# The last eight merge gates in pairs, each pair by seven block products with mixed inputs and summed weights

## The chip, the cores and the metric

The kernel runs on one core of a Trainium2 chip. The metric is the time of one execution on the device in microseconds (us). The core has one matmul engine (PE, with its weight loads shown apart as PEld), a vector engine (DVE), an activation engine (ACT), a general engine (POOL) and a queue engine (SP), on which this kernel starts nearly all of its transfers. Each engine works through its own list of instructions in order and waits for the others by semaphores.

## The reference

One layer of a hybrid decoder on 576 tokens (512 of a prompt, 64 of eight sampled sequences), all in 32-bit floats, D = 1024. What matters here:

```python
z = rmsnorm(x, norm1_g) @ w_in            # (576, 1024) @ (1024, N_IN)
# z holds the inputs of both branches and, at its end, 2 x 1024 columns of gates
y_a = mlstm_branch(z) @ w_branch_m        # (576, 512) @ (512, 1024)
y_b = rwkv_branch(z) @ w_branch_r         # (576, 512) @ (512, 1024)
gates = sigmoid(z[..., G_START:])
merged = gates[..., :D] * y_a + gates[..., D:] * y_b
x = x + merged @ w_out
u = rmsnorm(x, norm2_g) @ f_up            # then a convolution, gelu, f_down, ...
```

The gates are sixteen tiles of 128 columns: eight for y_a and eight for y_b. The sigmoid is made from tanh(z/2): the kernel stores tanh(z/2) and later takes (tanh + 1) * y, with a factor of one half.

## The kernel before, in words

**Layout and products.** Activations lie transposed: 128 channels on the partitions, the 576 tokens along the free axis, in two halves of 288 columns (HF). A matrix of 1024 input channels is eight blocks of 128. PE multiplies in a shortened 32-bit type (fp32r), so each operand is split into a high part and a remainder: the high part `wh` of a weight tile by a cast on ACT (L169), the remainder `wl` by a subtraction on DVE (L170), and the same for activations (names ending in h and l). Each product is three matmuls, wh by xh, wh by xl and wl by xh (half_k, L190 to L193). `dense` (L174) makes one output tile of 128 columns: it loads the weights as two tiles of 128x512 (L168), splits them, and issues for each of the two halves 8 blocks x 3 = 24 matmuls into a PSUM bank `pd`.

**Seven products for eight.** In the later stage f_up (`up`, L1316 and on) two output tiles are made together by `seven` (L287). Two tiles, with their inputs taken in upper and lower four blocks and the two column halves, are a product of 2x2 blocks by 2x2 blocks, eight block products in the plain way. `seven` makes seven, with weights that are sums of weight tiles (`plus`, L298) and activations that are mixed from the four quarter blocks (`mixed`, L274), and additions on the results. Each block product is 4 blocks x 3 = 12 matmuls (L306), so a pair takes 84 matmuls instead of 96. `seven` leaves the last product to its caller as `last`, so that a caller can read a bank before it.

**The gates.** `gate(i)` (L1205) makes gate i with `dense` from the normalised input `xs1` (tiles xa0h, xa0l to xa7h, xa7l), takes tanh of half of it on ACT into a tile `gst`, and stores that to DRAM as d_th[i] (L1210). An even i is a gate of y_a, an odd one a gate of y_b.

**What sets the order.** PLAN (L31) is a string of steps, and the body is issued in its order: x, a, d, b, s, c are steps of the RWKV branch (the last is c3, whose last results are stored to d_y[4] to d_y[7] at L941), m0 to m3 the four mLSTM heads, g0 to g15 the gates, which give PE dense work between the steps of the branches. A scheduler then reorders the instructions by its own estimate of when operands are ready, and fixes a list for each engine. The tail of PLAN is "... g7 m3 g8 g9 ... g15": the eight last gates stand behind the last head m3, whose products and vector work run among them. In a head, products of weights and values (L1136) are copied to `hn` (L1137), normalised in a chain of small DVE operations (L1154 and around) and ACT operations (L1156), transposed back on PE (L1159), multiplied into `og` and stored to d_y[h]. Then come the matrices of the sampled sequences (tiles C0 and VS, L1183 to L1203).

**Behind the gates.** `load_split` (L1230) reads d_y[4] to d_y[7] back as `yin` (L1232) and splits each (ACT L198, DVE L199) into y0h, y0l to y3h, y3l. `gated` (L1235) makes the branch's product with `dense` (four blocks, 24 matmuls), reads d_th as `th` (L1238) and multiplies. First come the eight tiles of y_b from d_y[4] to d_y[7], then the eight of y_a from d_y[0] to d_y[3], each added to its partner: that is the merge.

**Memory.** `rp` is the RWKV part's pool, `mp` the mLSTM part's, `wp` that of the weights (six raw tiles `wr`, four of wh and of wl). A tag names a place, and a new tile in a tag waits until the former one's readers are done.

Of the kernel before, what the change touches and what calls it, by code (L numbers as in the profile page):

```python
# [15 lines left out]
P = 128  # L16
# [11 lines left out]
KSC = 128.0 ** -0.5  # L28
DEC = math.exp(-0.5)

PLAN = "x0 a0 d0 x1 b0 a1 d1 s0 c0 g0 m0 b1 g1 x2 a2 d2 s1 c1 m1 g2 b2 x3 a3 d3 g3 s2 c2 b3 g4 g5 s3 m2 g6 c3 g7 m3 g8 g9 g10 g11 g12 g13 g14 g15".split()  # L31


VEC = {}
# [61 lines left out]
def build(tc, nc, I, O):  # L96
    from contextlib import ExitStack

    V, S, G, TE, SY = nc.vector, nc.scalar, nc.gpsimd, nc.tensor, nc.sync
# [9 lines left out]
    with st0:  # L109
# [32 lines left out]
        def half(hf):  # L142
            return slice(hf * HF, (hf + 1) * HF)
# [127 lines left out]
            return xn  # L271


        def mixed(tiles, pl, b11, b12, b21, b22, k, T4):  # L274

            n1, n2, t3, n4 = (pl.tile([P, HF], F32, tag=t, name="tt", bufs=2) for t in ("u2", "u2", "u3", "u3"))
            V.tensor_tensor(n1, b11, b12, ALU.subtract)
            G.tensor_tensor(t3, b22, b12, ALU.subtract)
            V.scalar_tensor_tensor(n2, n1, -1.0, b22, ALU.mult, ALU.subtract)
            V.tensor_tensor(n4, n2, b21, ALU.add)  # L280
            for name, t, e in (("n2", n2, V), ("n1", n1, G), ("t3", t3, V), ("n4", n4, V)):
                h, l = (tiles[name + a][:, k, :] for a in "hl")
                S.copy(h, t)
                e.tensor_tensor(l, t, h, ALU.subtract)
                T4[name].append((h, l))

        def seven(srca, srcb, x4, sp):  # L287

            def parts(w):
                wh, wl = [wp.tile([P, 4, P], F32R, tag=t, name=t, bufs=WB) for t in ("wh", "wl")]
                S.copy(wh, w)  # L294
                V.tensor_tensor(wl, w, wh, ALU.subtract)  # L295
                return wh, wl

            def plus(a, b, e):  # L298
                t = sp.tile([P, 4, P], F32, tag="ws", name="ws", bufs=3)
                e.tensor_tensor(t, a, b, ALU.add)  # L300
                return t

            def prod(pm, w, xs, more=False):
                for k in range(4):
                    for i, (a, b) in enumerate(((0, 0), (0, 1), (1, 0))):
                        TE.matmul(pm[:, 0:HF], w[a][:, k, :], xs[k][b], start=not more and k == 0 and i == 0,  # L306
                                  stop=k == 3 and i == 2, skip_group_check=more)

            def tile(tag):
                return sp.tile([P, HF], F32, tag=tag, name=tag, bufs=2)  # L310

            a11, a21, a22, a12 = wdma8(srca, 0), wdma8(srcb, 0), wdma8(srcb, 4), wdma8(srca, 4)
            A, F, E, Dm = (bank("d", "pd") for _ in range(4))
            w11 = parts(a11)
            prod(A, w11, x4["b11"])
            u3 = tile("u3")
            S.copy(u3, A[:, 0:HF])
            s1 = plus(a21, a22, V)
            s2 = plus(s1, a11, V)
            prod(F, parts(s2), x4["n2"])  # L320
            u2 = tile("u2")
            V.tensor_tensor(u2, F[:, 0:HF], u3, ALU.add)
# [12 lines left out]
            return A, u2, E, Dm, u3, last  # L335
# [40 lines left out]
        with ExitStack() as stn:  # L376
# [44 lines left out]
            xr = []  # L421
# [44 lines left out]
        rp = pool(stR, "rwkv")  # L466
# [11 lines left out]
        m0 = mp.tile([4, NB], F32, name="m0")  # L478
# [43 lines left out]

        xwa = r_tile(12, "t1")
        S.activation(xwa[0:64, :], xwa[0:64, :], AF.Tanh)
        xw = rp.tile([P, T], F32R, name="xw")
        xa = rp.tile([P, T], F32R, name="xa")
# [678 lines left out]
        def gate(i):  # L1205
# [3 lines left out]
                S.activation(th[:, hf * HF:(hf + 1) * HF], pss[hf][:, 0:HF], AF.Tanh, scale=0.5)  # L1209
            SY.dma_start(d_th[i], th)  # L1210

        mlstm_rows()
        for step in PLAN:
            (rwkv_in, rwkv_prep, rwkv_diag, rwkv_mid, rwkv_smp, rwkv_out, mlstm_head, gate)["xadbscmg".index(step[0])](int(step[1:]))
        SY.dma_start(O["o_shift"], o_shift)
        SY.dma_start(O["o_mconv"], o_mconv)

# [5 lines left out]
        x1 = [rpool.tile([P, T], F32, name=f"res{m}") for m in range(8)]  # L1223
# [43 lines left out]
        xn0 = [kp.tile([P, HF], F32, name=f"xn0{k}") for k in range(KD)]  # L1267
# [25 lines left out]
        fp = pool(stf_, "ffn")  # L1293
# [22 lines left out]
        def up(j):  # L1316
# [68 lines left out]
        for m in range(2):  # L1385
            hl = [fp.tile([P, 8, P], F32R, tag="x4", name="wg", bufs=8) for _ in range(2)]
# [133 lines left out]
```

## Time and profile before

| | |
|---|---|
| three runs | 1074.89, 1079.7, 1078.46 us; median 1078.46 |
| the profiled execution | 1070.66 us, of which the span of instructions is 1068.8 us |
| mean granted clock of PE in it | 0.996 |
| PE busy | 1045.1 us (98%), 8991 matmuls |
| DVE busy | 777.0 us (73%) |
| ACT busy | 508.8 us (48%) |
| POOL busy | 254.5 us (24%) |
| DMA | 114.74 MB, a mean of 107 GB/s |

The page gives a span, the busy time of each engine with the number of its instructions, and the chain of work that ended last, followed back from the end. A row of a group reads: line, engine, operation, output <- inputs, partitions x elements, count, then busy time and the mean of one in ns, then the time for which the engine stood idle ahead of it and what ended that. A row of the timeline reads: start in us, duration, engine, line, operation; a number in square brackets is the wait ahead of it. The granted clock is 1.00 at full speed.

### The profile page before, as it was taken

The numbers are of one execution on the slowest core, as the hardware profiler recorded it, in microseconds if no ns is written. First come the engines' busy times: TensorE is split into PE (matmuls) and PEld (weight loads), VectorE is DVE, ScalarE is ACT, GpSimd is POOL, SyncE is SP. The second block draws the span as 40 slices with busy tenths as digits, with TensorE's granted clock in tenths as the row PEclk, the third lists the DMA queues.
The fourth block names the chain that finished last, engine by engine and source line by source line (L and its number), as shares of the span: only waits on it lengthen the run. The fifth ranks groups of instructions, "written<-read, shape, count | busy, mean of one in ns | idle before, by whom it ended". The sixth has DMA issues, their size and how long they took to land.

```text
span 1068.8 us, 23108 instructions
## 1 busy us (share of the span) xinstructions
PE 1045.1 (98%) x8991; PEld 1009.0 (94%) x8991; DVE 777.0 (73%) x1645; ACT 508.8 (48%) x1072; POOL 254.5 (24%) x394
## 2 busy tenths in 40 slices
PE   8899999999999999999999999999999999999996
PEld 7899999999989988999999999999999999999996
DVE  7887657876786676356775799945998569975864
ACT  7684634462553344334343465522565236553822
POOL 7622112221131021001401253200343005410300
PEclk9999999999999999999999999999999999999999
DMA  7243412442342322446850312322233322342513
GB/s 252 95 127 93 108 53 58 103 141 60 88 143 75 81 84 91 143 151 234 263 181 1 116 37 93 110 90 75 85 99 97 102 70 90 94 117 67 165 40 123
DMA packets 90894, 114.74 MB, mean 107 GB/s; under 512 B 35617, under 2 KB 45217, under 8 KB 90785
## 3 DMA queue, kind: packets, MB, share of 16 engines
q1 hardware_dynamic: 90784, 113.27, 34.7%
q8 instruction: 70, 1.15, 0.4%
q14 instruction: 40, 0.32, 0.1%
HBM read 94.79 MB, written 18.45 MB: 106 GB/s over the span
## 4 chain that ended last, share of the span: by engine, by line
PE 90%; DVE 4%; DMA 4%; ACT 1%; issue 1%; SPq 0%; POOLq 0%; DVEq 0%; ACTq 0%
PE pd L193 55%; PE pd L306 20%; PE pm L655 1%; PE pm L1106 1%; PE pm L1136 1%; PE pm L835 1%; PE pm L809 1%; DMA yin<-d_y 1%; PE pm L910 1%; DVE xnf L268 1%; PE pm L917 1%; PE pm L1199 1%; PE pm L775 0%; DMA d_y<-og 0%; DMA wr<-i_w_out 0%
## 5 line engine op out<-in xcount | busy, mean ns | idle before, releaser
L169 ACT CAST wh<-wr 128x512 fp32r<-128x512 f32 (+2 forms) x170 | 101.7, 599 | 173.4 <-PE pd L193 140.7
L170 DVE TENSOR_TENSOR wl<-wr,wh 128x512 fp32r<-128x512 f32 (+2 forms) x170 | 118.8, 702 | 82.4 <-ACT wh L169 80.8
L193 PE MATMUL pd<-actl,wh 128*128 128x288 f32 x384 | 111.9, 295 | 0.0
L193 PE MATMUL pd<-acth,wl 128*128 128x288 f32 x384 | 111.4, 295 | 0.0
L193 PE MATMUL pd<-acth,wh 128*128 128x288 f32 x384 | 110.3, 295 | 0.0
L193 PEld LDWEIGHTS pd<-actl,wh 128*128 128x128 f32 x384 | 71.8, 188 | 0.0
L193 PEld LDWEIGHTS pd<-acth,wl 128*128 128x128 f32 x384 | 71.6, 188 | 0.0
L193 PEld LDWEIGHTS pd<-acth,wh 128*128 128x128 f32 x384 | 71.1, 188 | 0.1
L294 ACT CAST wh<-ws 128x512 fp32r<-128x512 f32 x76 | 47.1, 619 | 48.9 <-PE pd L306 24.8
L295 DVE TENSOR_TENSOR wl<-ws,wh 128x512 fp32r<-128x512 f32 x76 | 58.1, 765 | 8.4 <-ACT wh L294 7.9
L300 POOL TENSOR_TENSOR ws<-wr 128x512 f32<-128x512 f32 x19 | 31.7, 1670 | 96.9 <-DVE wl L295 54.1
L294 ACT CAST wh<-wr 128x512 fp32r<-128x512 f32 x57 | 35.3, 619 | 38.5 <-PE pd L306 24.0
L1333 POOL COPY o_f<-u 128x2 f32<-128x2 f32 x22 | 26.6, 1209 | 110.8 <-DVE u L1330 109.2
L295 DVE TENSOR_TENSOR wl<-wr,wh 128x512 fp32r<-128x512 f32 x57 | 39.5, 693 | 7.3 <-ACT wh L294 7.2
L216 POOL TENSOR_TENSOR rsc<-rsc,nhalf 128x3 f32<-128x3 f32 x8 | 9.3, 1167 | 131.1 <-DVE rsc L235 131.1
L1342 DVE SCALAR_TENSOR_TENSOR y<-u,vec,y 128x592 f32<-128x592 f32 x44 | 38.5, 875 | 1.2 <-ACT y L1340 1.0
L253 ACT ACTIVATE sq<-res 128x288 f32<-128x288 f32 x40 | 17.7, 445 | 36.0 <-DVE res L1279 18.5
L193 PE MATMUL pd<-mgh,ol 128*128 128x288 f32 x112 | 33.0, 296 | 0.0
L193 PE MATMUL pd<-mgl,oh 128*128 128x288 f32 x112 | 33.0, 295 | 0.0
L193 PE MATMUL pd<-mgh,oh 128*128 128x288 f32 x112 | 32.8, 295 | 0.0
L1370 DVE TENSOR_TENSOR res<-res,pd 128x288 f32<-128x288 f32 x48 | 20.9, 450 | 15.7 <-PE pd L193 15.5
L193 PE MATMUL pd<-xa0h,wh 128*128 128x288 f32 x86 | 26.4, 307 | 3.0 <-ACT zr L352 1.6
(825 smaller groups left out, 3949.4 us busy)
## 6 DMA issues: line engine op xcount, KB each, us to landing
wr<-i_w_in SPq DMA_DIRECT2D x92, 256.0 KB
wr<-i_f_up SPq DMA_DIRECT2D x88, 256.0 KB
wr<-i_f_down SPq DMA_DIRECT2D x32, 256.0 KB
d_th<-gst SPq DMA_DIRECT2D x16, 288.0 KB
th<-d_th SPq DMA_DIRECT2D x16, 288.0 KB
wr<-i_w_br SPq DMA_DIRECT2D x16, 256.0 KB
wr<-i_w_out SPq DMA_DIRECT2D x16, 256.0 KB
wr<-i_ple_gate SPq DMA_DIRECT2D x16, 256.0 KB
```

Of the source, the lines that this page charges most:

```text
L169: S.copy(wh[:, 0:nk, :], wr[:, 0:nk, :])
L170: V.tensor_tensor(wl[:, 0:nk, :], wr[:, 0:nk, :], wh[:, 0:nk, :], ALU.subtract)
L193: TE.matmul(pm[:, 0:HF], w[:, k % 4, :], a[:, c], start=k == 0 and i == 0, stop=k == n - 1 and i == 2)
L253: S.activation(sq, x[:, c], AF.Square)
L268: V.scalar_tensor_tensor(xn, xt[k][:, c], vcol(gname, k), rs, ALU.mult, ALU.mult)
L294: S.copy(wh, w)
L295: V.tensor_tensor(wl, w, wh, ALU.subtract)
L300: e.tensor_tensor(t, a, b, ALU.add)
L306: TE.matmul(pm[:, 0:HF], w[a][:, k, :], xs[k][b], start=not more and k == 0 and i == 0, stop=k == 3 and i == 2, skip_group_check=more)
L1333: G.tensor_copy(o_f[:, j, 0:2], u[:, TP:TP + 2])
L1342: V.scalar_tensor_tensor(y, u[:, i:i + 592], w(i), y, ALU.mult, ALU.add)
L1370: V.tensor_tensor(x1[m][:, c], x1[m][:, c], pss[hf][:, 0:HF], ALU.add)
```

## The change

PLAN's tail "m3 g8 g9 g10 g11 g12 g13 g14 g15" becomes "m3 t0 p4 p5 p6 p7". Step t0 is `mix_x`: it forms the mixed operands of `seven` from xs1. For each of four k it adds high part and remainder of the blocks k and k + 4 back together (one sum on DVE, one on POOL, 576 columns, into tag zr), and calls `mixed`, which takes four differences and sums of 288 columns, casts each on ACT and subtracts on DVE and POOL. The results (n1, n2, t3, n4, each high and remainder, for four k) lie in thirteen tiles in places of the RWKV part whose tiles are done by then (tags t2 to t5, xr, xk, xv, xw, xa, bon, AR, BK); the temporaries take the gates' own place gst. A step p, `gate_pair(p)`, makes gates 2p and 2p + 1 together: tile 16 + p as the first and 24 + p as the second of a pair in `seven`. The weight sums go to the places G0, G1 and UV in turn. The results are put together with additions on DVE and tanh on ACT, into two tiles gst, and stored, first d_th[2p + 1], then d_th[2p]; the second of these ends with the last addition.

`seven` and `mixed` take their places from their callers now (`halves`, `wsum`, `at`, `tmp`), and in the gates, where `turn` is empty, the fourth bank is one of tag r. In the f_up stage the same tiles as before are used.

```diff
-PLAN = "... m3 g8 g9 g10 g11 g12 g13 g14 g15".split()
+PLAN = "... m3 t0 p4 p5 p6 p7".split()
...
-        def seven(srca, srcb, x4, sp):
+        def seven(srca, srcb, x4, halves, wsum):
...
-            A, F, E, Dm = (bank("d", "pd") for _ in range(4))
+            A, F, E, Dm = (bank(t, "pd") for t in ("d", "d", "d", "d" if turn else "r"))
+            u2, u3 = halves()
...
+        def mix_x(_):
...
+            for k in range(4):
+                xk = []
+                for e, (h, l) in zip((V, G), (xs1[k], xs1[k + 4])):
+                    t = rp.tile([P, T], F32, tag="zr", name="xsum", bufs=2)
+                    e.tensor_tensor(t, h, l, ALU.add)
+                    xk += [t[:, half(0)], t[:, half(1)]]
+                mixed(lambda n, k: at[n, k & 2][:, k & 1, :], tmp, *xk, k, x4m)
...
+        sums = ["G0", "G1", "UV"]
+
+        def seven_mid(ja, jb):
...
+            def wsum():
+                sums.append(sums.pop(0))
+                return rp.tile([P, 4, P], F32, tag=sums[-1], name="ws")
...
+        def gate_pair(p):
+            b1, u2, b2, b3, u3, last = seven_mid(16 + p, 24 + p)
+            ta, tb = (mp.tile([P, T], F32, tag="gst", name="gst", bufs=2) for _ in range(2))
+            h0, h1 = half(0), half(1)
+            S.activation(ta[:, h0], b1[:, 0:HF], AF.Tanh, scale=0.5)
+            V.tensor_tensor(tb[:, h1], b2[:, 0:HF], u3, ALU.add)
+            last()
+            V.tensor_tensor(tb[:, h0], b3[:, 0:HF], u3, ALU.subtract)
+            S.activation(tb[:, h0], tb[:, h0], AF.Tanh, scale=0.5)
+            S.activation(tb[:, h1], tb[:, h1], AF.Tanh, scale=-0.5)
+            SY.dma_start(d_th[2 * p + 1], tb)
+            V.tensor_tensor(ta[:, h1], b2[:, 0:HF], u2, ALU.add)
+            S.activation(ta[:, h1], ta[:, h1], AF.Tanh, scale=0.5)
+            SY.dma_start(d_th[2 * p], ta)
```

How this moves instructions shows at two places. The first is SP's queue at the end of the gates, where the branch inputs are read back (yin of d_y4 to d_y7 for the first products, of d_y0 to d_y3 for the later ones); before, at the store of gate 14:

```order
L941 DMA d_y7_100<-bon_4310 128x576
L168 DMA wr_6948<-i_w_br 128x512
L1232 DMA yin_6706<-d_y4_97 128x576
L1232 DMA yin_6712<-d_y5_98 128x576
L1232 DMA yin_6718<-d_y6_99 128x576
L1232 DMA yin_6724<-d_y7_100 128x576
L1238 DMA th_6762<-d_th1_74 128x576
...
L1210 DMA d_th14_87<-gst_6599 128x576
```

And now:

```order
L1259 DMA d_th15_88<-gst_6792 128x576
L937 DMA d_y7_100<-bon_4310 128x576
L168 DMA wr_7196<-i_w_br 128x512
L1284 DMA yin_7169<-d_y0_93 128x576
L1284 DMA yin_7175<-d_y1_94 128x576
L1284 DMA yin_7181<-d_y2_95 128x576
L1262 DMA d_th14_87<-gst_6791 128x576
L1284 DMA yin_6851<-d_y4_97 128x576
L1284 DMA yin_6857<-d_y5_98 128x576
```

The reads of d_y4 to d_y7 have moved from ahead of gate 14's store to right behind it, and the reads of d_y0 to d_y2 from behind it to ahead of it.

The second place is PE at the passage from the gates (inputs xa) to the branch products (inputs y). Before, the transposes of head 3 (hn) come after a whole product and a half of the branch:

```order
L193 MATMUL pd<-xa7l,wh 128x288
L193 MATMUL pd<-xa7h,wl 128x288
L193 MATMUL pd<-y0h,wh 128x288
L193 MATMUL pd<-y0l,wh 128x288
...
L1159 MATMUL pm<-cst,hn 128x128
L193 MATMUL pd<-y0h,wl 128x288
```

And now, where L1132 is head 3's last product of weights and values (L1136 before) and L1155 its transposes:

```order
L306 MATMUL pd<-xa7l,wh 128x288
L306 MATMUL pd<-xa7h,wl 128x288
L1132 MATMUL pm<-V_0_2221,E 128x129 x4
L193 MATMUL pd<-y0h,wh 128x288 x7
L1155 MATMUL pm<-cst,hn 128x128 x2
L193 MATMUL pd<-y0l,wh 128x288
```

Head 3's last product has moved behind the last gate product (before, 29 matmuls of gate 15 followed it), its transposes stand seven matmuls behind it, and the branch begins with seven matmuls of y0h alone, for four products at once.

More of the change, by code (lines that the diff above doesn't have):

```diff
@@ L29 @@
 DEC = math.exp(-0.5)
-PLAN = "x0 a0 d0 x1 b0 a1 d1 s0 c0 g0 m0 b1 g1 x2 a2 d2 s1 c1 m1 g2 b2 x3 a3 d3 g3 s2 c2 b3 g4 g5 s3 m2 g6 c3 g7 m3 g8 g9 g10 g11 g12 g13 g14 g15".split()
+PLAN = "x0 a0 d0 x1 b0 a1 d1 s0 c0 g0 m0 b1 g1 x2 a2 d2 s1 c1 m1 g2 b2 x3 a3 d3 g3 s2 c2 b3 g4 g5 s3 m2 g6 c3 g7 m3 t0 p4 p5 p6 p7".split()
 VEC = {}
@@ L271, in norm_tile, with mixed @@
             return xn
-        def mixed(tiles, pl, b11, b12, b21, b22, k, T4):
-            n1, n2, t3, n4 = (pl.tile([P, HF], F32, tag=t, name="tt", bufs=2) for t in ("u2", "u2", "u3", "u3"))
+        def mixed(at, tmp, b11, b12, b21, b22, k, T4):
+            n1, n2, t3, n4 = tmp()
             V.tensor_tensor(n1, b11, b12, ALU.subtract)
@@ L281, in mixed @@
             for name, t, e in (("n2", n2, V), ("n1", n1, G), ("t3", t3, V), ("n4", n4, V)):
-                h, l = (tiles[name + a][:, k, :] for a in "hl")
+                h, l = (at(name + a, k) for a in "hl")
                 S.copy(h, t)
@@ L298, in plus @@
             def plus(a, b, e):
-                t = sp.tile([P, 4, P], F32, tag="ws", name="ws", bufs=3)
+                t = wsum()
                 e.tensor_tensor(t, a, b, ALU.add)
@@ L320, in seven @@
             prod(F, parts(s2), x4["n2"])
-            u2 = tile("u2")
             V.tensor_tensor(u2, F[:, 0:HF], u3, ALU.add)
@@ L524, in build @@
         S.activation(xwa[0:64, :], xwa[0:64, :], AF.Tanh)
-        xw = rp.tile([P, T], F32R, name="xw")
-        xa = rp.tile([P, T], F32R, name="xa")
+        xw = rp.tile([P, T], F32R, tag="xw", name="xw")
+        xa = rp.tile([P, T], F32R, tag="xa", name="xa")
         S.copy(xw[0:64, :], xwa[0:64, :])
@@ L1210, in gate, with tmp @@
             SY.dma_start(d_th[i], th)
+        x4m = {n: [] for n in ("n1", "n2", "t3", "n4")}
+        def mix_x(_):
+            at = {}
+            free = []
+            for t, b, n in [(t, 1, 1) for t in ("t2", "t3", "t4", "t5", "xr", "xk", "xv", "xw", "xa")] + [("bon", 2, 1), ("AR", 2, 2), ("BK", 1, 2), ("AR", 2, 2)]:
+                tl = rp.tile([P, n, 2, HF], F32R, tag=t, name="x4m", bufs=b)
+                free += [tl[:, i] for i in range(n)]
+            for k in (0, 2):
+                for n in ("n2", "n1", "t3", "n4"):
+                    for a in "hl":
+                        at[n + a, k] = free.pop(0)
+            def tmp():
+                a, b = (mp.tile([P, 2, HF], F32, tag="gst", name="tt", bufs=2) for _ in range(2))
+                return a[:, 0], a[:, 1], b[:, 0], b[:, 1]
+            for k in range(4):
[5 more added lines that the diff above has]
+                mixed(lambda n, k: at[n, k & 2][:, k & 1, :], tmp, *xk, k, x4m)
+            for n, k0, hf in (("b11", 0, 0), ("b21", 4, 0), ("b22", 4, 1)):
+                x4m[n] = [tuple(t[:, half(hf)] for t in xs1[k]) for k in range(k0, k0 + 4)]
@@ new lines, in build, with halves @@
+        sums = ["G0", "G1", "UV"]
+        def seven_mid(ja, jb):
+            def halves():
+                t = rp.tile([P, 2, HF], F32, tag="zr", name="hh", bufs=2)
+                return t[:, 0], t[:, 1]
+            def wsum():
+                sums.append(sums.pop(0))
+                return rp.tile([P, 4, P], F32, tag=sums[-1], name="ws")
+            return seven(I["w_in"][RT + ja], I["w_in"][RT + jb], x4m, halves, wsum)
+        def gate_pair(p):
[12 more added lines that the diff above has]
+            SY.dma_start(d_th[2 * p], ta)
@@ L1212, in build @@
         mlstm_rows()
         for step in PLAN:
-            (rwkv_in, rwkv_prep, rwkv_diag, rwkv_mid, rwkv_smp, rwkv_out, mlstm_head, gate)["xadbscmg".index(step[0])](int(step[1:]))
+            (rwkv_in, rwkv_prep, rwkv_diag, rwkv_mid, rwkv_smp, rwkv_out, mlstm_head, gate, mix_x, gate_pair)["xadbscmgtp".index(step[0])](int(step[1:]))
         SY.dma_start(O["o_shift"], o_shift)
@@ L1306, in build, with half_tiles, wsum @@
         x4 = {n: [] for n in ("n1", "n2", "t3", "n4")}
+        def half_tiles(*tags):
+            return lambda: [fp.tile([P, HF], F32, tag=t, name="tt", bufs=2) for t in tags]
+        def wsum():
+            return fp.tile([P, 4, P], F32, tag="ws", name="ws", bufs=3)
         xt4 = {n + a: fp.tile([P, 4, HF], F32R, tag="x4", name=n + a, bufs=8) for n in x4 for a in "hl"}
@@ L1310, in build @@
         for k in range(4):
-            mixed(xt4, fp, xn0[k], xn1[k], xn0[k + 4], xn1[k + 4], k, x4)
+            mixed(lambda n, k: xt4[n][:, k, :], half_tiles("u2", "u2", "u3", "u3"), xn0[k], xn1[k], xn0[k + 4], xn1[k + 4], k, x4)
         stK.close()
@@ L1324, in up @@
             else:
-                b1, u2, b2, b3, u3, last = seven(I["f_up"][j], I["f_up"][NFF + j], x4, fp)
+                b1, u2, b2, b3, u3, last = seven(I["f_up"][j], I["f_up"][NFF + j], x4, half_tiles("u2", "u3"), wsum)
                 V.tensor_tensor(ac[:, HF:T], b2[:, 0:HF], u3, ALU.add)
```

3 lines of the change are left out of this document (removed).

## The prediction, made before the changed kernel was run

> **What bounds the kernel now.** I read the page's shares and chain first, then one table of stages, then the waits of PE, then the single matmuls and the handover from the gates to the branch products.
>
> ```profile
> span 1068.8 us, 23108 instructions
> PE 1045.1 (98%) x8991; PEld 1009.0 (94%) x8991; DVE 777.0 (73%) x1645; ACT 508.8 (48%) x1072; POOL 254.5 (24%) x394
> PE 90%; DVE 4%; DMA 4%; ACT 1%; issue 1%; SPq 0%; POOLq 0%; DVEq 0%; ACTq 0%
> ```
>
> PE carries 90% of the chain. The next table has span length, PE, PEld, DVE, ACT, POOL busy (x instructions), granted clock, DMA share and GB/s. Gates 8 to 15 run from 418.7 to 485.3, the first branch products from 485.3 to 513.9; the stretch from 600 is the one where seven-product tiles already run.
>
> ```profile
> core 0: us, PE busy (x) PEld busy (x) DVE busy (x) ACT busy (x) POOL busy (x), PEclk, DMA share, GB/s
> 353.00:418.70 65.70, 64.20 (x764) 58.14 (x763) 46.85 (x119) 28.90 (x72) 9.82 (x19) 1.00 0.31 88
> 418.70:485.30 66.60, 66.60 (x557) 63.80 (x556) 31.41 (x69) 22.86 (x49) 5.67 (x11) 1.00 0.45 149
> 485.30:513.90 28.60, 27.31 (x208) 27.10 (x208) 18.85 (x42) 10.63 (x20) 5.96 (x8) 1.00 0.68 222
> 600.00:640.00 40.00, 38.45 (x288) 37.98 (x289) 36.86 (x71) 23.89 (x50) 20.35 (x26) 1.00 0.16 55
> 640.00:700.00 60.00, 59.61 (x449) 59.38 (x449) 56.47 (x108) 32.69 (x58) 18.37 (x24) 1.00 0.33 102
> ```
>
> In the gate stage PE is never idle and DVE is under half full, so a matmul less there is time less. One wait of the branch stage will matter below; the second row is that of the seven-product tiles:
>
> ```profile
> PE pd L306 <- DVE wl L295: 1.5, 2, 1.0
> PE pm L1199 <- DVE VS L1183: 1.3, 1, 1.3
> ```
>
> **The matmuls.** A matmul's busy time overlaps its neighbours, so its price is the distance between starts. PE's timeline of one dense product, first and last of 23 rows:
>
> ```profile
> 386.05 0.29 PE L193 MATMUL pd<-xa2h,wl 128*128 128x288 f32 x1
> ...
> 388.96 0.29 PE L193 MATMUL pd<-xa6h,wh 128*128 128x288 f32 x1
> ```
>
> 22 steps in 2.91 us are 0.1323 us each. A gate takes 2 halves x 8 blocks x 3 = 48 matmuls, two gates 96; a pair by seven block products takes 7 x 12 = 84. Four pairs save 48 matmuls, 48 x 0.1323 = 6.35 us. The new form costs no more per matmul, as a group of each form shows:
>
> ```profile
> L193 PE MATMUL pd<-xa3h,wl 128*128 128x288 f32 x16 | 4.7, 295 | 0.0
> L306 PE MATMUL pd<-t3h,wl 128*128 128x288 f32 x20 | 5.9, 295 | 0.0
> ```
>
> So 6.35 us (0.6% of 1078) is the whole prize; half a percent, 5.4 us, is about what a measurement of this kernel can tell from no change.
>
> **The work added beside PE.** Groups of DVE and ACT work (mean ns behind the busy time), the first four of the seven-product stage, the last two of the gates:
>
> ```profile
> L295 DVE TENSOR_TENSOR wl<-ws,wh 128x512 fp32r<-128x512 f32 x18 | 13.9, 774 | 0.1
> L295 DVE TENSOR_TENSOR wl<-wr,wh 128x512 fp32r<-128x512 f32 x13 | 8.8, 678 | 0.0
> L300 DVE TENSOR_TENSOR ws<-ws,wr 128x512 f32<-128x512 f32 x8 | 5.4, 679 | 0.0
> L322 DVE TENSOR_TENSOR u<-pd,u 128x288 f32<-128x288 f32 x5 | 2.2, 443 | 0.0
> L170 DVE TENSOR_TENSOR wl<-wr,wh 128x512 fp32r<-128x512 f32 x15 | 10.3, 688 | 15.8 <-ACT wh L169 15.2 <-PE pd L193 0.6
> L1209 ACT ACTIVATE gst<-pd 128x288 f32<-128x288 f32 x15 | 6.1, 408 | 9.7 <-PE pd L193 9.6
> ```
>
> A pair costs DVE 4 x 0.774 + 3 x 0.678 (splits) + 3 x 0.679 (weight sums) + 5 x 0.443 (additions on results) = 9.4 us, four pairs 37.5; the 16 splits that go gave 11.0. The stage's DVE rises from 31.4 to about 58, plus 3.5 of the mixing (8 operations of 0.443 stand behind its products' start): 61.5 in 66.6 - 6.35 = 60.2 us. Successive DVE operations overlap a little, so this is nearly full, not over: the load of the rows 600 (92%) and 640 (94%), where PE lost 1.55 of 40 and 0.39 of 60. For 60 us that is 0.4 to 2.3 us of PE waits; I take 1.2. The likeliest place is the first pair: its second weight sum goes where head 3's matrices lay, and they are read until shortly before.
>
> The rest of the mixing on DVE (4 blocks of six 0.443 and one sum of 576 columns, 0.76 by the split below, 13.7 us less 3.5) lands in the row 353, whose DVE goes from 47 to 57 of 65.7. Its cover is the head's own PE work; I cost it at nothing, with -1 to +2 us if it shifts waits there. ACT's 12 further casts and POOL's sums have more room still; the weights loaded are the same 16 x 2 tiles.
>
> **The handover.** The change puts more behind the last product, as the two pieces of the order shown with the change say. On SP's queue the branch inputs (yin of d_y4 to d_y7), before read three rows and more ahead of gate 14's store, now stand right behind it; and gate 14 has become the last pair's last result, so that its store waits for the very last product, an addition and a tanh, and the four reads queue behind it. On PE head 3's last value product and its transposes (hn) have moved together, with seven matmuls between them; before, 29 matmuls of gate 15 and 38 of the branch filled this distance, 67 x 0.1323 = 8.9 us. What lies between, in before's timeline (start, duration):
>
> ```profile
> 475.35 1.85 SPq L1232 DMA_DIRECT2D yin<-d_y  x4
> 478.55 0.67 ACT L198 CAST y0h<-yin 128x576 fp32r<-128x576 f32 x1 [0.53 <-DMA yin<-d_y]
> 483.43 0.76 DVE L199 TENSOR_TENSOR y3l<-yin,y3h 128x576 fp32r<-128x576 f32 x1
> 480.53 1.05 PE L1136 MATMUL pm<-V,E 128*128 128x129 f32 x8
> 483.30 0.26 ACT L1137 COPY hn<-pm 128x129 f32<-128x129 f32 x1
> 489.66 2.04 ACT L1156 ACTIVATE hn<-hn,hr,hsc 128x128 f32<-128x128 f32 x5 [3.39 <-DVE hr L1154]
> 490.30 0.27 PE L1159 MATMUL pm<-cst,hn 128*128 128x128 f32 x1
> ```
>
> Call T the end of the last gate product. Reads: addition 0.44, tanh 0.41, store and issue some 0.8, landing 3.2 (475.35 to 478.55), cast 0.67: the first y matmul at about T+5.5. Head: 1.05 for the product, then from hn's copy to the transpose 490.30 - 483.30 = 7.0: T+8.1, or T+9.8 counted from the product's end in before (481.58 to 490.30). In that time PE has the product and seven matmuls, 1.05 + 0.93 = 2.0. It idles 6.1 to 7.8 us; I take 6.5, with 3.5 below (only the reads binding) and 8.5 above. Then the other y splits are in, as ACT has them right behind hn's activations.
>
> Against that, the wait of 1.3 us (L1199 for VS) goes: it came because DVE stood for the last y of head 3, and the branch products now run later against that chain.
>
> **Sum**: -6.35 + 1.2 + 6.5 - 1.3 = 0.05, no change. The profiled execution took 1070.66 us (span 1068.8), below the median of 1078.46; the difference is put on the median: 1078.5 us, its own range 1075 to 1082.
>
> **Rivals.**
> The clock falls in the gap. Twice idle with seven matmuls between is more than any wait of this trace past the start (longest listed above 1.5). The start shows the price:
>
> ```profile
> 8.00:12.00 4.00, 3.15 (x14) 1.99 (x12) 3.68 (x5) 4.00 (x12) 2.81 (x4) 1.00 0.99 340
> 12.00:16.00 4.00, 3.69 (x15) 3.32 (x15) 4.00 (x5) 3.99 (x11) 3.88 (x4) 0.57 1.02 331
> 16.00:20.00 4.00, 4.00 (x33) 4.00 (x32) 4.00 (x10) 3.73 (x10) 2.94 (x4) 1.00 0.94 316
> ```
>
> After sparse work the clock stood at 0.57 and 15 matmuls ran where 33 run: 18 x 0.1323 = 2.4 us. That gives 1080.9. [...]
>
> The handover costs little (1 us): head 3's chain ends early, because its copy no longer stands behind y casts. Then -6.35 + 1.2 + 1 - 1.3 gives 1073.0, faster. For it: POOL is nearly free; against: both the reads and the chain would have to shrink.
>
> DVE becomes the stage's bound. Without overlap its 61.5 us at the 92% of row 600 take 66.8, so 6.6 us of waits take the place of 1.2 and 1083.9 follows, slower; it decides once splits come later than PE's twelve matmuls (1.6 us) on average. Against it: row 640, where 94% cost 0.39.
>
> The order of rows ahead of the gates changes as well (PE's differs from head 2 on); that could give 3 us either way without the gates being the cause.
>
> **How the numbers follow.** Forecast 0.45; clock 0.20; little handover 0.15; DVE 0.15; earlier order 0.05. Faster by over 0.5%: 0.11 of the little handover, 0.03 of the forecast (a gap of 3.5 and no DVE wait already give -4.2), 0.02 of the earlier order, 0.16. Slower: 0.10 of DVE, 0.05 of the clock with a gap at its upper end, 0.03 of the forecast, 0.02 of the earlier order, 0.20. The rest, 0.64, is the same. The range goes from 1071.5 (the little handover without the 1.2 of waits, and a little) to 1085.0 (DVE's case with a longer gap by 1.1), leaving about 0.08 out below and 0.1 above.
>
> **What would show it.** Right: 6.35 us fewer matmuls by the count of L193 and L306; PE idle twice between the last L306 and the branch, ended by ACT (y0h, then hn), some 6 us together; hardly any wait of L306 on DVE; no L1199 wait. Wrong: idle there under 2 us, or PE waiting for wl at each pair with DVE full.

## The result, and the profile after

The changed kernel is slower: 1093.16 us (median of 4, 1090.7 to 1094.94) against 1076.87 us of the kernel before beside it, a ratio of 1.0169 (95% interval 1.0142 to 1.0195). No change had been forecast, and the time lies above the range. The profiled execution took 1092.25 us, its span 1090.5 us, 21.7 us more than that of before. The page of the changed kernel:

```profile
span 1090.5 us, 23159 instructions
PE 1052.5 (97%) x8943; PEld 1013.4 (93%) x8943; DVE 820.6 (75%) x1717; ACT 523.4 (48%) x1104; POOL 276.8 (25%) x410
...
PEclk9999999999979989998999999999999999999998
```

The last of these rows, the granted clock in 40 slices, was in the kernel before:

```profile
PEclk9999999999999999999999999999999999999999
```

Two subtractions divide the 21.7 us. PE stood idle for 1068.8 - 1045.1 = 23.7 us before and for 1090.5 - 1052.5 = 38.0 now: 14.3 more. It was busy for 7.4 us more, with 48 matmuls (6.35 us) fewer: 13.7 us in which the same work took longer. The rows of the clock say why: there are slices of 7 and 8 where before every slice had 9. By the records of the granted clock in the trace, the changed kernel ran at half clock from 299.0 to 316.0, from 391.1 to 397.9 and from 503.8 to 510.6, 30.7 us together. In the first of them dense products start 0.24 us apart (313.9 to 315.8 us), at full clock 0.13 us (from 510.7 us on); so the three hold an estimated 15.4 us of lost work at most, half their length, and less where PE was idle. A table by stretches shows the places; its columns are those of the prediction's tables (span length, busy time of PE, PEld, DVE, ACT, POOL, granted clock, DMA):

```profile
280.00:298.00 18.00, 13.96 (x156) 12.86 (x155) 11.89 (x32) 7.31 (x21) 3.68 (x4) 1.00 0.47 118
298.00:316.00 18.00, 18.00 (x139) 14.01 (x138) 8.83 (x18) 2.98 (x7) 3.34 (x6) 0.53 0.31 90
316.00:386.00 70.00, 70.00 (x758) 64.67 (x756) 51.30 (x121) 32.16 (x76) 15.50 (x27) 1.00 0.30 85
386.00:398.00 12.00, 7.63 (x60) 6.64 (x60) 11.80 (x21) 4.59 (x11) 6.92 (x6) 0.72 0.24 61
398.00:436.60 38.60, 38.15 (x486) 33.71 (x486) 32.06 (x73) 18.09 (x44) 12.87 (x19) 1.00 0.21 68
436.60:498.00 61.40, 60.28 (x503) 56.91 (x502) 51.69 (x108) 30.73 (x63) 13.29 (x14) 1.00 0.42 135
498.00:514.60 16.60, 9.32 (x57) 9.12 (x57) 10.12 (x21) 8.39 (x18) 3.55 (x5) 0.79 0.70 241
514.60:535.60 21.00, 21.00 (x162) 21.00 (x161) 13.76 (x29) 6.07 (x10) 2.86 (x4) 1.00 0.73 223
```

Gates 8 to 15 run from 436.6 to 498.0: 61.4 us where they took 66.6, as forecast. But they begin 17.9 us later than before (418.7), and the way from their end to the first merge product, 28.6 us before, takes 37.6 (to 535.6). So the account is +17.9 - 5.2 + 9.0 = 21.7 us. The waits of PE name three new long ones, and one that has grown (the two rows of TT are two transfers of the same kind; the wait for `warm` of 2.8 us at the start, which every version has, is left out):

```profile
PE pd L193 <- ACT y0h L198: 7.3, 1, 7.3
PE pm L771 <- DMA TT<-scr0t: 3.0, 2, 2.8
...
PE pm L771 <- DMA TT<-scr1t: 2.2, 1, 2.2
PE pm L870 <- DVE Xs L866: 2.2, 1, 2.2
```

The first is the handover. The second (near 294 us) lies 140 us ahead of the gates and is followed by 18 us at a clock of 0.53. Before, it was:

```profile
PE pm L775 <- DMA TT<-scr0t: 1.5, 1, 1.5
```

The others, at 386 and 390, lie in 12 us at a mean clock of 0.72.

At 390, the timeline of DVE shows who is in the way of Xs, a copy of 0.28 us in the chain of the RWKV branch:

```profile
386.91 0.86 DVE L279 SCALAR_TENSOR_TENSOR tt<-tt,xsum 128x288 f32<-128x288 f32 x1
387.69 1.34 DVE L1230 TENSOR_TENSOR xsum<-xa2h,xa2l 128x576 f32<-128x576 f32 x1
388.96 0.45 DVE L280 TENSOR_TENSOR tt<-tt,xsum 128x288 f32<-128x288 f32 x1
389.33 2.02 DVE L284 TENSOR_TENSOR x4m<-tt,x4m 128x288 fp32r<-128x288 f32 x2
391.27 0.68 DVE L170 TENSOR_TENSOR wl<-wr,wh 128x512 fp32r<-128x512 f32 x1
391.87 0.28 DVE L866 COPY Xs<-pm 128x128 f32<-128x128 f32 x1
```

The products that Xs copies had ended by 384.1 us. Four rows of the mixing (five operations) and a weight split stand ahead of it without a pause, and one sum of 576 columns took 1.34 us where its neighbours took 0.72 and 0.75.

### The profile page after: what moved, and what is told of

Its sections match the earlier page's. It is cut to its first block, busy times and chain, and to the rows that moved or that the text cites. A ratio compares the mean times of both kernels' runs of the same rounds, so it can differ in the third digit from the quotient of the medians.

```text
span 1090.5 us, 23159 instructions
## 1 busy us (share of the span) xinstructions
PE 1052.5 (97%) x8943; PEld 1013.4 (93%) x8943; DVE 820.6 (75%) x1717; ACT 523.4 (48%) x1104; POOL 276.8 (25%) x410
## 5 line engine op out<-in xcount | busy, mean ns | idle before, releaser
L169 ACT CAST wh<-wr 128x512 fp32r<-128x512 f32 (+2 forms) x154 | 91.9, 598 | 162.1 <-PE pd L193 137.7
L170 DVE TENSOR_TENSOR wl<-wr,wh 128x512 fp32r<-128x512 f32 (+2 forms) x154 | 104.9, 685 | 60.7 <-ACT wh L169 59.1
L294 ACT CAST wh<-ws 128x512 fp32r<-128x512 f32 x92 | 56.9, 619 | 63.5 <-PE pd L306 33.1
L295 DVE TENSOR_TENSOR wl<-ws,wh 128x512 fp32r<-128x512 f32 x92 | 69.6, 758 | 9.3 <-ACT wh L294 8.5
L300 POOL TENSOR_TENSOR ws<-wr 128x512 f32<-128x512 f32 x23 | 38.3, 1666 | 117.5 <-DVE wl L295 75.2
L294 ACT CAST wh<-wr 128x512 fp32r<-128x512 f32 x69 | 42.7, 619 | 49.1 <-PE pd L306 32.5
L295 DVE TENSOR_TENSOR wl<-wr,wh 128x512 fp32r<-128x512 f32 x69 | 49.0, 709 | 9.2 <-ACT wh L294 9.1
L300 DVE TENSOR_TENSOR ws<-ws,wr 128x512 f32<-128x512 f32 x46 | 31.7, 688 | 2.8 <-PE pm L831 2.5
L1429 DVE TENSOR_TENSOR res<-res,pd 128x288 f32<-128x288 f32 x48 | 20.9, 451 | 15.6 <-PE pd L193 15.5
```

Of the source, the lines that this page charges most:

```text
L169: S.copy(wh[:, 0:nk, :], wr[:, 0:nk, :])
L170: V.tensor_tensor(wl[:, 0:nk, :], wr[:, 0:nk, :], wh[:, 0:nk, :], ALU.subtract)
L1429: V.tensor_tensor(x1[m][:, c], x1[m][:, c], pss[hf][:, 0:HF], ALU.add)
```

## The experiments

**1. The parts apart.** Theory A after the result: the loss comes from the mixing, by the rows that it moves ahead of it and by its DVE work among chains that PE waits for. Theory B: it comes from the pairs and the handover.

`mix_only` keeps t0 and makes the gates plain:

```diff
-... g7 m3 t0 p4 p5 p6 p7
+... g7 m3 t0 g8 g9 g10 g11 g12 g13 g14 g15
```

> The mixing step t0 stays, and gates 8 to 15 are plain dense products again (the mixed operands are made and not used). Up to about 370 us its lists of instructions are those of the changed kernel, the sum of xa0h and xa0l hoisted to 247 us included. Theory A (the loss comes from the mixing: the rows it moves ahead of it, and its own DVE and POOL work in the middle of head 3 and c3, with PE waits of over 2 us after which the clock falls): clock at half from about 300 to 316 us as in the changed kernel, waits for TT and Xs near 386 to 390; gate 8 begins 12 to 18 us later than in before; no wait for y0h; the whole 10 to 18 us slower than before. Theory B (the loss comes from the pairs and the handover): within 3 us of before.

Ratio 1.0127 (1.0094 to 1.0160), with the waits of the changed kernel and none for y0h (`warm` is the wait at the start):

```profile
PE pm L771 <- DMA TT<-scr0t: 3.3, 2, 3.0
PE pm L390 <- ACT warm L387: 2.8, 1, 2.8
PE pm L771 <- DMA TT<-scr1t: 2.3, 1, 2.3
PE pm L870 <- DVE Xs L866: 2.1, 1, 2.1
```

So three quarters of the loss (1.27 of 1.69%) come with operands that nobody reads: theory A.

`pairs_unmixed` keeps the pairs and drops t0:

```diff
-        x4m = {n: [] for n in ("n1", "n2", "t3", "n4")}
+        x4m = {n: [tuple(t[:, half(hf)] for t in xs1[k]) for k in range(k0, k0 + 4)]
+               for n, k0, hf in (("n1", 0, 1), ("n2", 4, 0), ("t3", 4, 1), ("n4", 0, 1), ...)}
-... m3 t0 p4 p5 p6 p7
+... m3 p4 p5 p6 p7
```

> The four pairs by seven products stay, step t0 goes: where seven wants mixed operands it gets plain quarters of the normalised input instead, so the gates' values are not the reference's and the time holds no mixing. Up to about 370 us its lists are those of before. Theory A: no fall of the clock ahead of the gates; the gate stage 4 to 6 us shorter; a wait for y0h of 4 to 7 us at the handover and some half-clock time behind it (2 us); in all -2 to +4 us against before. Theory B: 12 us or more of the 18 us remain.

Ratio 1.0009 (0.9993 to 1.0025): no change, the number that the prediction had for the whole. Its longest wait is the handover:

```profile
PE pd L193 <- ACT y0h L198: 5.2, 1, 5.2
```

`pairs_unmixed_6` takes three pairs, also unmixed, and ends with plain gates:

```diff
-... m3 p4 p5 p6 p7
+... m3 p4 p5 p6 g14 g15
```

> As pairs_unmixed (no mixing, gates not the reference's), with three pairs only and gates 14 and 15 as plain dense products at the end, so that nothing of the pair's end chain stands ahead of the branch inputs: 36 matmuls less than before, 4.8 us. If the wait for y0h came from the last pair's end, it is under 1 us now, and the time 3 to 5 us under before (ratio 0.995 to 0.997). If it came from DVE being full throughout (c3's last tile late), the wait stays at 3 to 5 us and the ratio is 0.998 to 1.003.

Ratio 0.9941 (0.9917 to 0.9965), no wait for y0h. A last pair in the place of two plain gates therefore costs 0.0068 of 1074 us, 7.3 us net (by the two intervals, some 4 to 10); with the 12 matmuls that it saves (1.6 us) the handover costs 8.9 us. The wait came from the last pair's end, not from a full DVE.

`plain_end` does the same to the changed kernel:

```diff
-... m3 t0 p4 p5 p6 p7
+... m3 t0 p4 p5 p6 g14 g15
```

> The changed kernel with p4 p5 p6 g14 g15 at the end: the mixing as it is, the last two gates plain. From pairs_unmixed and pairs_unmixed_6 the handover of a last pair costs 0.0068 of 1074 us, 7.3 us, net of its 1.6 us of matmuls. If this adds to the mixing's loss, the ratio is 1.007 to 1.011, with no wait for y0h over 1 us. If the handover is only where a delay of the mixing shows, it stays at 1.014 or more and the wait turns up elsewhere.

Ratio 1.0071 (1.0036 to 1.0107), as `mix_only` and `pairs_unmixed_6` add up to (1.27 - 0.59%); the waits for TT (2.9) and Xs (2.3) are still there.

**2. Moved rows or own time.** In the changed kernel's order the first sum of the mixing, xa0h + xa0l, is hoisted on DVE to about 247 us, since its inputs and its place (zr) are free then. `one_sum` adds to the kernel before only this sum and its partner on POOL:

```diff
-... g7 m3 g8 ...
+... g7 m3 t0 g8 ...
+        def one_sum(_):
+            for e, (h, l) in zip((V, G), (xs1[0], xs1[4])):
+                t = rp.tile([P, T], F32, tag="zr", name="xsum", bufs=2)
+                e.tensor_tensor(t, h, l, ALU.add)
```

> The kernel before, with one thing of the change alone: the first two sums of the mixing (xa0h + xa0l on DVE, xa4h + xa4l on POOL, results unused). Its lists are those of the changed kernel up to some 370 us, since the sum is hoisted to 247 us and moves rows behind it; nothing of the rest is there. Theory A1 (these moved rows cause the first loss): a wait for TT near 294 us of 2.8 to 3.0 us, half clock from 298 for 10 to 17 us, 6 to 10 us slower than before. Rival A2 (only the mixing's body near 380 us costs; the first loss is luck of one execution): within 2 us of before.

Ratio 1.0097 (1.0059 to 1.0135): two operations of 0.75 and 1.4 us that nobody reads cost 10 us. A table of `one_sum` at the place:

```profile
280.00:296.70 16.70, 13.15 (x152) 12.45 (x152) 11.01 (x34) 7.68 (x22) 2.32 (x3) 0.99 0.46 113
296.70:317.00 20.30, 20.29 (x144) 16.02 (x145) 8.83 (x18) 3.29 (x8) 3.34 (x6) 0.51 0.27 92
```

`dead_small` puts a smaller sum (128x128) at the same place; the scheduler then leaves the lists as they were, but for two small groups on PE:

```diff
+            t = rp.tile([P, T], F32, tag="zr", name="xsum", bufs=2)
+            V.tensor_tensor(t[:, 0:P], xs1[0][0][:, 0:P], xs1[0][1][:, 0:P], ALU.add)
```

> The kernel before with one unused sum of 128x128 on DVE at the place to which the change's first sum is hoisted (row 397 of DVE, about 247 us). SP, ACT and POOL lists are those of before, DVE's has the one row more, on PE two small groups change places. If moved rows are the cost of one_sum, this costs nothing: ratio 0.998 to 1.002. If DVE work at that place is what costs, it is 1.003 or more.

Ratio 0.9999 (0.9984 to 1.0015). The same two stretches:

```profile
280.00:296.70 16.70, 16.10 (x202) 14.01 (x201) 11.39 (x29) 7.48 (x20) 0.72 (x3) 1.00 0.63 169
296.70:317.00 20.30, 20.30 (x250) 18.73 (x249) 16.75 (x35) 11.78 (x24) 9.20 (x13) 0.92 0.34 106
```

250 matmuls where `one_sum` ran 144, in the same 20.3 us with PE busy in both. What TT waits for shows in the last step of its chain, 30 small DVE operations ahead of a copy to Td, which is stored and read back as TT; this copy in the kernel before, `one_sum` and `dead_small`:

```profile
284.81 0.37 DVE L746 COPY Td<-Qd 72x256 f32<-72x256 f32 x1
289.19 0.38 DVE L746 COPY Td<-Qd 72x256 f32<-72x256 f32 x1
284.97 0.38 DVE L746 COPY Td<-Qd 72x256 f32<-72x256 f32 x1
```

In `one_sum` the chain begins 2.5 us later (274.98 for 272.52) and ends 4.4 us later, as rows have moved on DVE and PE; two of them, a weight split and a product with og (0.69 and 0.68 us), stand ahead of the chain's last product and stood behind it before. `dead_pool` adds the POOL sum alone, with all other lists unmoved:

```diff
+            t = rp.tile([P, T], F32, tag="zr", name="xsum", bufs=2)
+            G.tensor_tensor(t, *xs1[4], ALU.add)
```

> The kernel before with one unused sum of 128x576 on POOL alone (1.4 us), all other lists unmoved. By the moved rows: ratio 0.998 to 1.002. If POOL's work slowing DVE at that place is what costs, 1.003 or more.

Ratio 1.0000 (0.9982 to 1.0018). So an added operation that moves next to no rows is free here (0.28 us on DVE, 1.74 us on POOL), and the rows that `one_sum` moves are what is left. Its DVE sum of 0.75 us in unmoved lists was not run.

**3. What makes the clock fall.** `clock_ladder` chained gates 8 to 15 so that PE should wait ahead of gates 9, 11, 13 and 15 (tanh and 0, 2, 4 and 6 copies before a write to the gate's bank):

```diff
+                for _ in range(n or 0):
+                    t = mp.tile([P, HF], F32, tag="lad", name="lad", bufs=2)
+                    S.copy(t, first)
+                    first = t
+                for pm in pss:
+                    S.copy(pm[:, 0:1], first[:, 0:1])
```

> The kernel before, with gates 8 to 15 chained so that PE must stand idle ahead of gates 9, 11, 13 and 15, for the tanh and 0, 2, 4 and 6 copies on ACT of some 0.4 us: gaps of about 1, 2, 3 and 4 us in dense work, nothing else changed. If a gap alone makes the clock fall, the rows behind the longer gaps show half the granted clock for some us and those behind the shorter ones do not, and the threshold lies between 1.8 us (the longest wait of before, without a fall) and 2.8 us (the wait for TT in the changed kernel, with one). The rival (sparse small matmuls make it fall, not the gap): no fall behind any of the four, as the work around them is dense.

It failed as an experiment: the scheduler filled the gaps with work of head 3 and the RWKV branch, and no wait in the ladder was over 1.8 us. One of 1.7 us (at 468.8) was followed by 3.4 us of half clock, but it stood among small products of head 3 and doesn't part the two. The question stays with the waits that the kernels have anyway. In the profiled executions, the four waits for TT near 294 us of 2.8 to 3.1 us (changed kernel, `mix_only`, `plain_end`, `one_sum`) were all followed by half clock, for 10.2 to 20.5 us; those of 1.0 us and less at this place had none right behind them; of the three of 1.3 to 1.5 us (before, `quiet_mix` and `quiet_mix_dve`, below) the latter two were followed by 3.4 and 6.8 us of it. A wait isn't needed either: `dead_small`, `dead_pool` and `pairs_unmixed_6`, none of them slower than before, ran at half clock for 3.4 us from 313 or 314 us on with PE busy throughout. What sets the loss apart is how long the half clock lasts: 3.4 us in these three, 20.5 in `one_sum`.

`one_sum_filled` fills the wait of `one_sum` with small useless products:

```diff
+            if p == 2:
+                pw, td = bank("s"), pairs[p]["Td"].rearrange("q s t -> q (s t)")
+                for _ in range(9):
+                    TE.matmul(pw[0:64, 0:256], td[:, 0:64], td, start=True, stop=True)
```

> one_sum with nine useless matmuls (64x256, some 0.5 us each, on Td, which is ready at about 289.5 us) put in front of the products that wait for TT near 294 us, so that PE is busy in what was a wait of 3.1 us. If the idle PE makes the clock fall and the half clock is what costs, the wait is under 1 us, the clock stays at 1.00 from 296 to 317 and the time falls by 6 to 10 us against one_sum in spite of the added work (ratio to before 0.999 to 1.004; one_sum had 1.0097). If the sparse small products behind the wait bring the half clock anyway, or if the moved rows cost by themselves, the ratio stays at 1.008 or more.

Ratio 1.0100 (1.0040 to 1.0161): three executions took 1088.91 to 1091.61 us at a clock of 0.981 or 0.982, the fourth 1078.12 at 0.994. The profile, of one of the three:

```profile
290.50:306.00 15.50, 14.85 (x62) 9.94 (x62) 2.60 (x9) 1.45 (x3) 0.43 (x2) 0.56 0.40 97
```

PE is busy there and has half clock all the same: being busy with a few 64x256 products did not hold it in this execution (`after_filled`, below, had it otherwise). `one_sum_dense` takes 45 of the gates' dense matmuls instead:

```diff
+                TE.matmul(pw[0:64, 0:256], td[:, 0:64], td, start=True, stop=True)
+                for _ in range(45):
+                    TE.matmul(pw[:, 0:HF], xs1[0][0][:, 0:P], xs1[1][0][:, 0:HF], start=True, stop=True)
```

> one_sum with 45 useless dense matmuls (128x128 by 288, 0.132 us each, 6.0 us) from 289.5 us on, in front of the products that wait for TT. If the half clock comes from PE standing idle or thinly used, the clock stays at 1.00 around 294, hardly any half clock follows up to 317 and the time is 4 to 8 us under one_sum in spite of 6 us of added work (ratio 1.002 to 1.006). If the thin products behind TT bring it in any case, half clock of 8 us or more remains between 296 and 317 and the ratio is 1.010 or more.

```profile
290.00:294.00 4.00, 3.74 (x14) 3.14 (x15) 0.53 (x3) 0.77 (x1) 0.44 (x2) 0.57 0.48 70
294.00:317.00 23.00, 23.00 (x261) 20.56 (x260) 14.72 (x35) 8.49 (x18) 3.21 (x9) 1.00 0.36 109
```

Ratio 1.0068 (1.0045 to 1.0091). The stretch to 317 us has the full clock again after a short fall, and by the ratios the kernel is some 3 us faster than `one_sum` with 6 us of work more, though the intervals overlap and it is short of the 4 to 8 us expected: another wait of 3.0 us has come up at 424 us, with 3.4 us of half clock behind it, so that the fill moved rows too. In these profiles the half clock lasted 20.5 us among the thin products of `one_sum` and 3.4 us where dense ones followed.

`after_filled` put fillers of both kinds into the changed kernel: nine small ones ahead of each wait for TT, as above, and six 128x512 products on hn at the handover.

```diff
+            if h == 3:
+                pw = bank()
+                for _ in range(6):
+                    TE.matmul(pw, hn[:, 3, 0:P], hn.rearrange("p i x -> p (i x)")[:, 0:512], start=True, stop=True)
```

> The changed kernel with useless matmuls at its three long waits: nine on Td ahead of each wait for TT (294 and 386 us), six 128x512 on hn behind head 3's last product (499 us). The wait for Xs near 390 stays. If the falls of the clock hold 10 to 15 of the 18 us, the ratio comes from 1.017 to 1.003 to 1.009, with hardly any half clock behind 294 and 506 us. If the waits themselves hold them, it stays at 1.013 or more.

Ratio 1.0161 (1.0113 to 1.0208): no gain. The profiled execution had 3.4 us of half clock near 385 us and none at the other places (clock 0.994) and took 1088.3 us, the others 1092 to 1098 at 0.984 to 0.989. Of this the fillers and a wait for Xs of 3.0 us took their part; how much each took was not parted. The small fillers near 290 us (18 rows for the nine products), in `one_sum_filled` and then here:

```profile
291.15 7.89 PE L777 MATMUL pm<-Td 72*64 72x256 f32 x18 [0.76 <-DVE Td L746]
289.87 4.10 PE L773 MATMUL pm<-Td 72*64 72x256 f32 x18 [0.75 <-DVE Td L742]
```

The same products behind the same wait ran at half clock there and at full clock here. So whether such products hold the clock differs from one execution to another, and these runs don't settle it.

**4. Another place for the mixing.** `mix_late` holds the sums until c3 frees G0 and G1:

```diff
-... m3 t0 p4 p5 p6 p7
+... m3 g8 g9 t0 p5 p6 p7
-                    t = rp.tile([P, T], F32, tag="zr", name="xsum", bufs=2)
+                    t = rp.tile([P, T], F32, tag=("G0", "G1")[e is G], name="xsum")
```

> PLAN ends m3 g8 g9 t0 p5 p6 p7, and the sums of the mixing lie in places that c3 frees (G0, G1), so that the mixing cannot run ahead of c3's end; three pairs instead of four (36 matmuls less than before, 4.8 us). Theory A: lists as before up to about 385 us, no fall of the clock until the gates, the handover as in the changed kernel (7 us idle, 2 to 3 us of clock, less 1.3): +1 to +5 us against before. Theory B, and the rival that DVE cannot take the mixing beside the gates wherever it stands: +10 us or more, with PE waiting for wl or for mixed operands between 410 and 480 us.

Ratio 1.0217 (1.0187 to 1.0247): theory A's number failed. The loss ahead of 385 us is gone, but the mixing now stands in head 3's way, and the clock is at half for 23.9 us from 446 us on:

```profile
PE pm L1102 <- DVE E L1103: 5.1, 3, 2.7
PE pm L1105 <- DVE E L1103: 3.0, 1, 3.0
```

`mix_dve` is `mix_only` with POOL's share of the mixing on DVE:

```diff
-        def mixed(at, tmp, b11, b12, b21, b22, k, T4):
+        def mixed(at, tmp, b11, b12, b21, b22, k, T4, G=G):
...
-                for e, (h, l) in zip((V, G), (xs1[k], xs1[k + 4])):
+                for e, (h, l) in zip((V, V), (xs1[k], xs1[k + 4])):
...
-                mixed(lambda n, k: at[n, k & 2][:, k & 1, :], tmp, *xk, k, x4m)
+                mixed(lambda n, k: at[n, k & 2][:, k & 1, :], tmp, *xk, k, x4m, V)
```

> As mix_only (mixing, plain gates, operands unused), with the mixing's work on POOL moved to DVE: 4 sums of 0.76, 8 operations of 0.44, 6.6 us more on DVE and 15 us less on POOL. If the loss near 385 us comes from DVE and POOL slowing each other (sums of 0.75 us take 1.3 to 1.95 beside POOL's), the waits for Xs and TT there shorten to under 1.5 us and the whole is 3 to 8 us faster than mix_only. If it is the amount of DVE work in a chain, the waits grow and it is as slow or slower.

Ratio 1.0209 (1.0176 to 1.0242), slower than `mix_only`. But its order is another from about 280 us on, and the wait for TT near 294 was 0.6 us in it, with half clock from 401.6 and from 500.6 us for 10.2 us each and a wait for y0h of 5.0 us, though its gates are plain. It shows only that sparing POOL did not help here, and that a wait for y0h can come without pairs too.

`quiet_mix` combines sums in G0 and G1 as in `mix_late`, temporaries in zr, plain gates ahead and behind:

```diff
-... m3 t0 p4 p5 p6 p7
+... m3 t0 g8 g9 p5 p6 g14 g15
-                a, b = (mp.tile([P, 2, HF], F32, tag="gst", name="tt", bufs=2) for _ in range(2))
+                a, b = (rp.tile([P, 2, HF], F32, tag="zr", name="tt", bufs=2) for _ in range(2))
```

> A version meant to be better than both: PLAN ends m3 t0 g8 g9 p5 p6 g14 g15; the sums lie in G0 and G1, so that the mixing starts behind c3, where DVE of before is busy 35% of the time, its temporaries in zr instead of the gates' own place; plain gates ahead of the pairs and behind them. 24 matmuls less, 3.2 us. Theory A: no fall of the clock ahead of the gates, no wait for y0h, -3 to +1 us against before. Rival (the mixing disturbs head 3 wherever it stands, as in mix_late): PE waits for E and Es of head 3 between 430 and 465 us, +5 us or more.

Ratio 1.0042 (1.0024 to 1.0059): PE waits for c3's step Sa (1.0, 1.9 and 1.2 us) and for V (1.4) between 443 and 454, and the clock is at half from 452 to 459 (the profiled execution is the slowest of its ten, 1083.69 us for a median of 1078.74). `quiet_mix_dve` does the mixing there on DVE alone, by the edit of `mix_dve` with the sums still in G0 and G1:

> quiet_mix with the mixing's POOL work on DVE. In quiet_mix operations of 0.44 us took up to 1.65 beside POOL's sums, and head 3's and c3's small steps (Sa) stood behind them: PE waited 5.5 us between 443 and 453. If the two engines slowing each other is the cost, the operations take 0.44 again, the waits halve and the ratio falls from 1.0042 to 0.997 to 1.001. If it is the number of DVE operations queued ahead of the chain's steps, the waits grow and the ratio is 1.005 or more.

Ratio 1.0025 (1.0001 to 1.0048). The intervals of the two overlap, so that which is faster stays open. The durations don't: the last subtraction of the mixing in `quiet_mix`, and then in `quiet_mix_dve`,

```profile
L284 DVE TENSOR_TENSOR x4m<-tt,x4m 128x288 fp32r<-128x288 f32 x12 | 8.9, 764 | 0.0
```

```profile
L284 DVE TENSOR_TENSOR x4m<-tt,x4m 128x288 fp32r<-128x288 f32 x16 | 7.0, 451 | 0.0
```

takes a mean of 764 ns with POOL's sums and 451 without them. In `quiet_mix` the three of the twelve that began while one of POOL's sums ran took 1.65 to 1.67 us, the other nine 0.44 to 0.54. In the changed kernel the same shows: during POOL's sums of 382.51 to 384.61 and 389.55 to 391.03 us, the subtractions that began at 383.46 and 389.70 took 1.46 and 1.65 us, and those at 385.99 and 392.27, with POOL idle, 0.44. None of the versions that compute everything is faster than the kernel before.

## Why the prediction was wrong, step by step

**The matmuls** (-6.35): right, 8943 for 8991. **The waits for DVE in the gate stage** (+1.2): the number was right, by luck; PE is busy 60.28 of 61.40 us, and the stage became 5.2 us shorter where 6.35 - 1.2 had been forecast, but the listed waits there are 0.7 us for head 3's C and 0.4 for a cast on ACT, none of L306 for DVE. DVE was busy 51.7 us of it (84%) instead of 61.5. The pairs' own DVE work was as forecast (36.3 us for 37.5); of the mixing 1.8 us stood in the stage instead of 3.5, and of other work some 14 instead of 20, the four y splits among what now came behind it. The rival of DVE as the bound did not come.

**The handover** (+6.5, less 1.3): the place was right, the two waits were one, of 7.28 us. In the changed kernel's timeline the last gate products end at 497.96:

```profile
497.96 1.05 PE L1132 MATMUL pm<-V,E 128*128 128x129 f32 x8
506.29 2.05 PE L193 MATMUL pd<-y0h,wh 128*128 128x288 f32 x7 [7.28 <-ACT y0h L198]
508.14 0.63 PE L1155 MATMUL pm<-cst,hn 128*128 128x128 f32 x2
...
497.57 1.47 SPq L1284 DMA_DIRECT2D yin<-d_y  x3
499.13 0.38 SPq L1262 DMA_DIRECT2D d_th<-gst  x1
499.57 2.59 SPq L1284 DMA_DIRECT2D yin<-d_y  x4
...
505.57 0.67 ACT L198 CAST y0h<-yin 128x576 fp32r<-128x576 f32 x1 [0.81 <-DMA yin<-d_y]
```

The first y matmul came at T + 8.3 instead of T + 5.5. The term that was too small is the landing: 3.2 us had been taken from before, and the first of the four reads, issued at 499.57, landed 6.0 us later, at 505.57. The reads of d_y0 to d_y2, which the order had put ahead of gate 14's store and the prediction did not count, went first; the transfer engines were 98% busy from 499.5 to 505.5, against 77% from 475.3 to 478.6, where before's reads landed, and ACT was done with the casts of those three 0.81 us before the read of d_y4 landed. Head 3's transposes at T + 10.2 then had no wait of their own, so that a sum of two waits came near the one that was there by luck. The wait for VS went as forecast. **The clock in the gap** (a rival, 2.4 us): it came, at half from 503.8 to 510.6, 4.3 us of it with PE busy, which loses an estimated 2 (dense products start 0.24 us apart up to 510.5, 0.13 from 510.7 on); the stretch to the merge grew by 9.0 us, near the 8.9 that the runs price the handover at. In this profile pairs and handover make -5.2 + 9.0 = 3.8 us; `pairs_unmixed`, whose wait for y0h was 5.2 us, shows 1.0 (-0.8 to 2.7). Its agreement with the forecast of no change owes something to chance, as the forecast had no fall of the clock and two waits. (The prediction's longest listed wait of 1.5 is two waits; the longest single one past the start was 1.8 us, at 1058.9.)

**The step that failed** is the mixing: "Its cover is the head's own PE work; I cost it at nothing, with -1 to +2 us", and with it the last rival, the earlier order at "3 us either way". Measured alone (`mix_only`) it costs 1.27%, 13.6 us, of which `one_sum` finds about 10 (6 to 14) in the rows moved by its first two sums. The timeline at 390 us shows the rest in kind, rows of the mixing ahead of Xs, but no run has it alone. Three things were not seen. The order had been read at the gates, not where it first differs: DVE's first other row is that sum, 190 us ahead of the stage. The share of DVE in a stretch was taken for its room, but PE there waits for single small operations in chains (the chain of TT ended 4.4 us later with 0.75 us more of work), and what counts is what is queued ahead of them. And the wait for TT stood in before's list with 1.5 us; that 1.3 us more (2.8) could be followed by 17.1 us at half clock was not considered there; the clock was priced for the handover alone.

**How much is clock.** Each execution has a time and a mean granted clock. Within the kernels (155 executions of the 16 that ran more than once, each taken from its kernel's mean) the time rises by 8 us for 0.01 of clock. Before has a median of 1074.3 us at 0.993 (61 executions beside the experiments, 1070.4 to 1081.2 us, clocks of 0.987 to 0.997), the changed kernel 1093.2 at 0.980: by this slope 0.013 of clock are an estimated 10 of the 19 us between the medians, the waits less the saved matmuls the rest. The profiled execution of before, with a clock of 0.996 and no half clock between 16 and 1040 us, was one of the good ones, which is why its span stood below the median.

What stays open: which of the moved rows lengthens the wait for TT was not tried alone, nor was the mixing near 390 us without its first sums. What the clock needs to fall is open: at the place of TT, waits up to 1.0 us had no fall right behind them and waits from 2.8 us had one in all four profiles, but falls came without a wait as well.

## What to carry to other kernels

Find where the order first differs before pricing the stage that the change names, and read what waits there: an unused operation of 0.75 us on DVE, with its partner on POOL, cost 1% with the rows that it moved, and one of 0.28 us that moved next to none cost nothing. Price a PE wait of 3 us ahead of thin products by the half clock behind it (10.2 to 20.5 us here behind the four waits for TT, with dense products starting 0.24 us apart instead of 0.13), not by its own length alone. Room on an engine is not its idle share: ask which small operation of a chain stands behind the new work, and whether the engine beside it slows it (a mean of 764 ns with POOL's sums and 451 without them, in `quiet_mix` and `quiet_mix_dve`).

## What the runs showed of the hardware

The granted clock fell to half behind waits that are short against its effect (20.5 us behind 3.1 us in `one_sum`), and PE being busy was not always enough to hold it: 62 products in 15.5 us at 0.56 in `one_sum_filled`, though the same fillers ran at full clock in `after_filled` (4.10 us for 7.89). In all 17 profiles every stretch of half clock between 20 and 640 us, and in ten of them between 20 and 1040 us, lasts 3.41 us or a whole multiple of it, up to seven times (23.9 us in `mix_late`); six of these steps followed the wait in `one_sum`, one stood at its place in `one_sum_dense`. From one execution of the same program to the next the mean clock differs (0.981 and 0.994 for `one_sum_filled`, 13 us apart). The falls at TT came behind waits of 1.3 to 3.1 us, the one in `dead_small` with PE busy for all of the 12 us around it (306 to 318 us); what decides whether and for how long the clock falls was not shown. A DVE operation of 0.45 us that began during a sum on POOL took 1.65 to 1.67 us in `quiet_mix`, 1.46 and 1.65 in the changed kernel.
